# A recurrence kept in flight for two chunks at once: grouping its small matrix products on TensorE

## The chip, the cores and the metric

The kernel runs on one core of one Trainium2 chip. The metric is the time of one execution on the device in microseconds (us). Five engines work side by side, each through its own queue in order: PE (TensorE, matrix products), DVE (VectorE), ACT (ScalarE), POOL (GpSimd) and SP (SyncE, which issues most transfers). PEld in a row is TensorE's loading of weights.

## The reference, cut to what matters

One layer of a diffusion backbone runs over 1024 latent and 128 context tokens of width 1024: a feed-forward half step, a token mixer, a second feed-forward half step, a last norm. The mixer has attention and, beside it, a gated linear recurrence (HGRN2) that runs forwards and backwards over the tokens in 8 heads of 64 keys and 64 values. Everything is float32.

```python
# S_t = diag(f_t) S_{t-1} + k_t outer v_t,  o_t = S_t^T q_t,  k_t = 1 - f_t, chunkwise
q_h = silu(hq);  f_fw = lb0 + (1 - lb0) * sigmoid(hf_f);  f_bw likewise
o_fw, s_fw = hgrn2_chunked(q_h, 1 - f_fw, log(f_fw), v_h, s0[:, 0])
o_bw, s_bw = hgrn2_chunked(flip(q_h), flip(1 - f_bw), flip(log(f_bw)), flip(v_h), s0[:, 1])
o_rec = rmsnorm(o_fw + flip(o_bw), hg_norm_g) * silu(hgate)
merged = sigmoid(ga) * (o_attn @ w_up_attn) + sigmoid(gr) * (o_rec @ w_up_rec)
```

## The kernel before

**The dense products.** A float32 product is made of three products of split operands (high and low parts: `xh`, `xl`, `wh`, `wl`; lines 454 to 456). In the mixer, `dense_g` makes one output tile of 128 rows by 384 tokens from eight blocks of the inner dimension, in two halves of 12 matrix products each, with a `yield` between. Such a half is the unit in which the rest is dealt out. All 1152 tokens are three chunks of 384 (`ORDER` is 2, 0, 1). The generators `proj_f`, `proj_q`, `proj_v`, `proj_gate` and `proj_sg` make the projections of the mixer: forget gates per head, queries, values and output gates per pair of heads, and sigmoid gates that go to memory.

**The recurrence.** Each head and chunk (24 in all) goes through two generators. `scan_pre` makes decays and scaled keys and queries (`Kb`, `Qb`, `KE`, `QP`) on DVE, ACT and POOL. `scan_lev` makes the part inside 128-token tiles by levels: first the products inside blocks of 8 (level 0, `Kb` with `Qb`), then a level for each m of 8, 16, 32, 64, in which keys of one half of a block of 2m meet queries of the other half. The forward direction lies on partitions 0 to 63, the backward one on 64 to 127. For m of 8 and 16, one product over all 128 partitions covers both directions, because `kr[m]` holds zeros where a direction has no keys. For level 0 and for m of 32 and 64 there are two products over 64 partitions, one for each direction, into two banks. After each level, `KE` (DVE) and `QP` (DVE for the backward direction, POOL for the forward one) are multiplied by the decays of that level, ACT copies the next keys into `kr`, and ACT or DVE moves the products out. Then come `kt` (the transposes of `KE`) and `dS` (the change of state). `scan_out` runs the state `S` over the nine tiles of a head on DVE and makes the outputs `po`. The products of the levels lie in three banks (tag `lv`), those of `kt`, `dS`, `po`, `vt` (transposed values) and `ops` (the norm of a pair's output) in three more (`sm`), and the dense ones in two (`mm`).

**The order.** A scheduler keeps close to the order in which the program is written. The main loop takes one chunk after the other and puts one half of a projection behind each step of `scan_lev`:

```python
for _ in self.scan_lev(d, b):
    next(work, None)      # a half of a projection: 12 dense products
    next(pre, None)       # a step of scan_pre for the next chunk
```

**The entry.** The first feed-forward step ends in `down_last`, chunk after chunk; the norm of the third chunk (`norm`, the generator `self.tail`) is still to be done when the mixer starts, and is dealt out between the first projections (`weave(feed(0))`). `mixer_consts` makes the constants of the mixer there, with a transfer of `mask` from ACT's queue.

Of the kernel before, what the change touches and what calls it, by code (L numbers as in the profile page):

```python
# [19 lines left out]
P = 128  # L20
# [6 lines left out]
CW = 384  # L27
# [61 lines left out]
class Trunk:  # L89
# [3 lines left out]
    def run(self):  # L93
        self.part, self.mode, self.chunks, self.bg = {}, "ffn1", ORDER, iter(())
        nc, tc, a = self.nc, self.tc, self.a
        with ExitStack() as st:
            self.cp = st.enter_context(tc.tile_pool(name="cp", bufs=1))
            self.wp = st.enter_context(tc.tile_pool(name="wp", bufs=1))
            self.tp = st.enter_context(tc.tile_pool(name="tp", bufs=25))
# [10 lines left out]
            with tc.tile_pool(name="mp", bufs=1) as mp:  # L110
                self.mixer_consts(mp)
                self.mixer()
# [268 lines left out]
    def norm(self, c, i):  # L381

        nc = self.nc
        lo, hi = span(c)
        cs = slice(lo, hi)
        rs = self.rs[:, cs]
        if self.mode != "mix":
            rs = self.bank("ps1", "rsp", hi - lo)
        self.stat_end(c, rs)
        yield  # L390
        for k in range(KT):
            t = self.fp.tile([P, hi - lo], F32, tag=self.nt[0], bufs=self.nt[1], name="xn")
            nc.vector.tensor_mul(t, self.x[k][:, cs], rs)
# [11 lines left out]
            nc.gpsimd.tensor_sub(tl, t, th)  # L405
            yield
# [205 lines left out]
    def mixer_consts(self, cp):  # L612
        nc, a = self.nc, self.a
        self.mask = cp.tile([P, 4, G], U8, name="mask")
        mf = self.tt(F32, "maskf")[:, : 4 * G]
        nc.scalar.dma_start(mf, a["mask"])
        nc.vector.tensor_copy(self.mask.rearrange("p a b -> p (a b)"), mf)
# [36 lines left out]
    def proj_f(self, i, h, out):  # L654
# [3 lines left out]
        w = self.load_w(self.a["w_in"][i], KT, P, home="pieces" if i == 0 else "low")  # L658
        for c in ORDER:
            s = self.sigm((yield from self.proj_g(w, c)))  # L660
            lo, hi = c * CW, (c + 1) * CW
            for r, o in ((slice(0, 64), 0), (slice(64, P), 1)):
                nc.scalar.activation(
                    fs[r, lo + o : hi + o], s[r], AF.Identity, scale=self.lb1[r, h : h + 1], bias=self.lb[r, h : h + 1]
                )
            yield

    def proj_q(self, i, out):
        q = out["q"] = self.tt(F32, "q")
        w = self.load_w(self.a["w_in"][i], KT, P, home="low")  # L670
        for c in ORDER:
            ps = yield from self.proj_g(w, c)
            self.nc.vector.tensor_mul(q[:, c * CW : (c + 1) * CW], ps, self.sigm(ps))  # L673
            yield

    def proj_v(self, i, out):
        nc = self.nc
        V = out["V"] = self.tt(F32, "V")
        w = self.load_w(self.a["w_in"][i], KT, P, home="low")
        for c in ORDER:  # L680
# [3 lines left out]
            pt = self.pp.tile([P, CW], F32, tag="sm", bufs=3, name="vt")  # L684
            for j in range(3):
                nc.tensor.transpose(pt[:, ts(j, P)], t[:, ts(j, P)], self.ident)
            nc.scalar.copy(V[:, c * CW : (c + 1) * CW], pt)
            yield

    def proj_gate(self, i, p, oT):  # L690
        nc = self.nc
        w = self.load_w(self.a["w_in"][i], KT, P, home="low")
        sq = self.tt(F32, "osq")[:, :T]
        nc.scalar.activation(sq, oT[:, :T], AF.Square)
        for c in ORDER:
            ps = yield from self.proj_g(w, c)
            if c == ORDER[0]:
                self.lnexp()
                for b in ORDER:
                    self.rec_norm(b, oT, sq)  # L700
            s = self.sigm(ps)
            nc.vector.tensor_mul(s, ps, s)
            cs = slice(c * CW, (c + 1) * CW)
            nc.gpsimd.tensor_mul(s, oT[:, cs], s)
            nc.sync.dma_start(self.orec[p][:, cs], s)
# [9 lines left out]
    def hgrn(self):  # L715
        nc = self.nc
# [9 lines left out]
        for t in self.XY:  # L726
            nc.vector.memset(t[:, :, 3:4], 1.0)
        for t in self.A1 + [self.A2, self.kr[8], self.kr[16]]:
            nc.vector.memset(t, 0.0)
        self.cnt = 0  # L730
# [11 lines left out]
        for i, _ in enumerate(weave(feed(0))):  # L742
            if i < 12:
                next(self.tail, None)
            if i == 11:
                assert next(self.tail, 1)
        def scan_of(h):
# [4 lines left out]
            d.update(pairs[p])  # L752
# [4 lines left out]
        def work_of(h):  # L757
            p = h // 2
            work = feed(h + 1) if h + 1 < H else []
            if h and h % 2 == 0:  # L760
                work = [self.proj_gate(5 * p - 1, p - 1, pairs[p - 1]["o"])] + work
            while len(work) < 4:
# [3 lines left out]
        d = scan_of(0)  # L766
        for _ in self.scan_pre(d, ORDER[0]):
            pass
        for h in range(H):
            work = work_of(h)  # L770
            for n, b in enumerate(ORDER):
                nd, pre = None, iter(())
                if n < NCH - 1:
                    pre = self.scan_pre(d, ORDER[n + 1])
                elif h + 1 < H:
                    nd = scan_of(h + 1)
                    pre = self.scan_pre(nd, ORDER[0])
# [7 lines left out]
            for _ in work:  # L785
                pass
            oT, d = d["o"], nd
        for _ in self.proj_gate(19, 3, oT):
            pass

# [3 lines left out]
    def scan_pre(self, d, b):  # L794
        nc = self.nc
        fs, q, QP, hh = d["f"], d["q"], d["QP"], d["h"] % 2
# [23 lines left out]
        Kb, Qb, KE = tmp("Kb", 2), tmp("Qb", 2), tmp("KE", 2)  # L820
# [20 lines left out]
    def scan_lev(self, d, b):  # L841
        nc = self.nc
        V, QP, hh, Gall = d["V"], d["QP"], d["h"] % 2, d["Gall"]
# [3 lines left out]
        if b == ORDER[0]:  # L847
            d["dS"] = self.fp.tile([P, 9, 64], F32, tag="dS", bufs=1, name="dS")
            S = d["S"] = self.fp.tile([P, 8, 64], F32, tag="S", bufs=1, name="S")
# [6 lines left out]
        Af = d["As"][b] = tmp("Af", 4, (P, 3, P))  # L856
# [5 lines left out]
        def products(parts, k, q, blocks):  # L862
            for j in range(3):
                kj, qj = k[:, ts(j, P)], q[:, ts(j, P)]
                for ki, qi in blocks:
                    for r, ps in parts:
                        ks, qs = (ki, qi) if r != B else (qi, ki)
                        n = qs.stop - qs.start
                        nc.tensor.matmul(ps[ks, j, :n], kj[r, ks], qj[r, qs], start=True, stop=True)
# [16 lines left out]
        for li, m in enumerate((8, 16, 32, 64)):  # L886
            kr = self.kr[m]
            if m < G:
                ps = lv()
                products([(slice(0, P), ps)], kr, qp, diag)  # L890
            else:
                pair = (A, lv()), (B, lv())
                blocks = [(slice(u, u + m), slice(u + m, u + 2 * m)) for u in range(0, P, 2 * m)]
                products(pair, kr, qp, blocks)
# [16 lines left out]
            else:  # L911
                for u, v in blocks:
                    nc.scalar.copy(Af[u, :, v], pair[0][1][u, :, :m])
                    nc.scalar.copy(Af[v, :, u], pair[1][1][v, :, :m])
# [12 lines left out]
        yield  # L927
        pd = self.pp.tile([P, 3, 64], F32, tag="sm", bufs=3, name="dS")
# [5 lines left out]
        yield  # L934

    def scan_out(self, d):
        nc = self.nc
        h, V, QP, Gall, S, dS = d["h"], d["V"], d["QP"], d["Gall"], d["S"], d["dS"]
# [8 lines left out]
        for pairs, lows, highs in (((3, 4), (2, 5)), (2, 4), (4, 6)), (((1, 6), (0, 7), (8,)), (0, 2), (6, 9)):  # L947
# [9 lines left out]
            for half, (t0, t1) in ((A, lows), (B, highs)):  # L957
                pv = po[half, : t1 - t0].rearrange("p a b -> p (a b)")
                nc.scalar.copy(d["o"][r, t0 * P : t1 * P], pv)
# [652 lines left out]
    def ffn_fast(self, l, gm, nxt):  # L1612
# [93 lines left out]
        if l == 0:  # L1706
            self.bg = self.ada_sum((6, 7), lambda: self.bank("up", "cb", D // 2), partial(self.tt, F32), self.slim)
# [133 lines left out]
```

## Time and profile before

| what | value |
|---|---|
| time, median of 3 runs | 2933.15 us (2932.75 to 2934.38) |
| time of the profiled execution | 2932.25 us, of which the span in the trace is 2930.1 us |
| PE busy in the span | 2833.2 us (97%) |
| DVE, ACT, POOL busy | 1976.7, 1285.9, 957.3 us |
| first projections of the mixer to the last of its recurrence | from about 832 to 1456 us of the span |

A busy time is the sum of what an engine's instructions took; the ends of matrix products are modelled and overlap, so what PE really needs for a piece of work is read from the starts of its products in the timeline. A granted clock (PEclk) below 1 means that TensorE was slowed for a part of the stretch.

### The profile page before, as it was taken

The numbers are of one execution on the slowest core, as the hardware profiler recorded it, in microseconds if no ns is written. First come the engines' busy times: TensorE is split into PE (matmuls) and PEld (weight loads), VectorE is DVE, ScalarE is ACT, GpSimd is POOL, SyncE is SP. The second block draws the span as 40 slices with busy tenths as digits, with TensorE's granted clock in tenths as the row PEclk, the third lists the DMA queues.
The fourth block names the chain that finished last, engine by engine and source line by source line (L and its number), as shares of the span: only waits on it lengthen the run. The fifth ranks groups of instructions, "written<-read, shape, count | busy, mean of one in ns | idle before, by whom it ended". The sixth has DMA issues, their size and how long they took to land. (4 is left out here: it accounts for less than half of the span.)

```text
span 2930.1 us, 54396 instructions
## 1 busy us (share of the span) xinstructions
PE 2833.2 (97%) x20946; PEld 2668.0 (91%) x20946; DVE 1976.7 (67%) x4282; ACT 1285.9 (44%) x2574; POOL 957.3 (33%) x904
## 2 busy tenths in 40 slices
PE   6999999999999999999998999999999999999998
PEld 5999999999988888888996877699999999999997
DVE  7677777677678777777357777856665665556665
ACT  6432323321176666666536777721552332232112
POOL 0133322444132122222145444532342222235431
PEclk9999999999999999999998999999999999999999
DMA  6643333643111111111200001242542322235211
GB/s 245 206 146 122 122 127 111 255 162 119 61 61 66 40 55 42 55 42 53 73 31 14 16 18 34 74 163 72 165 147 93 108 83 75 75 120 199 92 46 65
DMA packets 151492, 282.44 MB, mean 96 GB/s; under 512 B 19201, under 2 KB 83777, under 8 KB 151233
## 3 DMA queue, kind: packets, MB, share of 16 engines
q1 hardware_dynamic: 151088, 278.90, 27.8%
q8 instruction: 165, 2.70, 0.4%
q14 instruction: 95, 0.77, 0.1%
q10 hardware_dynamic: 144, 0.07, 0.0%
HBM read 215.37 MB, written 63.52 MB: 95 GB/s over the span
## 5 line engine op out<-in xcount | busy, mean ns | idle before, releaser
L1590 PE MATMUL b<-xo,wo 128*128 128x288 f32 x3552 | 484.6, 296 | 0.0
L1590 PEld LDWEIGHTS b<-xo,wo 128*128 128x128 f32 x3552 | 476.4, 188 | 0.0
L483 DVE SCALAR_TENSOR_TENSOR x<-dn,modt,x 128x256 f32<-128x256 f32 (+4 forms) x728 | 353.3, 505 | 169.0 <-PE dn L456 168.1
L454 PE MATMUL mm<-xh,wh 128*128 128x384 f32 (+1 forms) x1008 | 363.5, 361 | 5.7 <-DVE q L673 3.7
L1590 PE MATMUL b<-bh,wo 128*128 128x288 f32 x1776 | 366.4, 295 | 0.6 <-ACT et L1600 0.6
L456 PE MATMUL mm<-xh,wl 128*128 128x384 f32 (+1 forms) x1008 | 342.8, 340 | 0.3 <-DVE wl L228 0.2
L455 PE MATMUL mm<-xl,wh 128*128 128x384 f32 (+1 forms) x1008 | 342.3, 340 | 0.0
L1590 PEld LDWEIGHTS b<-bh,wo 128*128 128x128 f32 x1776 | 289.2, 188 | 0.9 <-ACT et L1600 0.9
L1590 PE MATMUL b<-bl,wo 128*128 128x288 f32 x888 | 261.9, 295 | 0.0
L243 POOL TENSOR_TENSOR wl<-raw,wh 128x1024 fp32r<-128x1024 f32 (+3 forms) x71 | 152.0, 2142 | 267.8 <-ACT wh L242 265.0
L1565 ACT CAST wo<-raw 128x512 fp32r<-128x512 f32 x185 | 114.7, 621 | 229.5 <-PE b L1590 119.3
L454 PEld LDWEIGHTS mm<-xh,wh 128*128 128x128 f32 (+1 forms) x1008 | 189.8, 188 | 19.6 <-DVE q L673 4.3
L1566 DVE TENSOR_TENSOR wo<-raw,wo 128x512 fp32r<-128x512 f32 x185 | 127.1, 688 | 104.8 <-ACT wo L1565 101.9
L454 PE MATMUL dn<-hh,wh 128*128 128x384 f32 (+2 forms) x576 | 196.2, 341 | 1.3 <-DVE et L1606 0.8
L456 PE MATMUL dn<-hh,wl 128*128 128x384 f32 (+2 forms) x576 | 194.6, 338 | 1.0 <-POOL wl L243 1.0
L455 PE MATMUL dn<-hl,wh 128*128 128x384 f32 (+2 forms) x576 | 194.2, 337 | 0.0
L455 PEld LDWEIGHTS mm<-xl,wh 128*128 128x128 f32 (+1 forms) x1008 | 190.4, 189 | 1.9 <-issue 0.4
L456 PEld LDWEIGHTS mm<-xh,wl 128*128 128x128 f32 (+1 forms) x1008 | 189.9, 188 | 1.8 <-DVE wl L228 0.5
L1668 POOL TENSOR_TENSOR hl<-hr,hh 128x1152 fp32r<-128x1152 f32 x44 | 118.0, 2693 | 194.5 <-ACT hh L1667 100.7
L314 DVE SCALAR_TENSOR_TENSOR junk<-wada,cb 128x512 bf16<-128x512 f32 x224 | 165.0, 737 | 7.1 <-DMA wada<-in_w_aT 6.3
L1322 POOL TENSOR_TENSOR ehl<-e,ehl 128x512 fp32r<-128x512 f32 x93 | 122.6, 1323 | 141.7 <-ACT ehl L1320 78.8
L1590 PEld LDWEIGHTS b<-bl,wo 128*128 128x128 f32 x888 | 167.4, 189 | 0.0
(391 smaller groups left out, 6904.2 us busy)
## 6 DMA issues: line engine op xcount, KB each, us to landing
raw<-in_w SPq DMA_DIRECT2D x148, 256.0 KB, 3.2
raw<-in_w SPq DMA_DIRECT2D x58, 512.0 KB, 3.5
wada<-in_w_aT SPq DMA_DIRECT2D x112, 256.0 KB, 2.9
hr<-hs SPq DMA_DIRECT2D x44, 576.0 KB, 5.2
hs<-et SPq DMA_DIRECT2D x148, 144.0 KB, 1.7
raw<-in_w_in SPq DMA_DIRECT2D x41, 512.0 KB, 3.2
hb<-hd SPq DMA_DIRECT2D x44, 288.0 KB, 3.5
x<-in_xT SPq DMA_DIRECT2D x16, 576.0 KB, 6.4
```

What stands on the lines that cost most here:

```text
L243: pin((eng or self.nc.gpsimd).tensor_sub(wl, raw, wh))
L314: nc.vector.scalar_tensor_tensor(junk, ws[n % 2], 1.0, cs[s], ALU.mult, ALU.mult, accum_out=o)
L454: pin(nc.tensor.matmul(ps, wh, xh, start=start and i == 0, stop=False))
L455: pin(nc.tensor.matmul(ps, wh, xl, start=False, stop=False))
L456: pin(nc.tensor.matmul(ps, wl, xh, start=False, stop=stop and i == n - 1))
L483: nc.vector.scalar_tensor_tensor(self.x[m][:, a:b], ps[:, a - lo : b - lo], self.modt[:, gm, m, s : s + 1], self.x[m][:, a:b], ALU.mult, A ...
L1322: eng.tensor_sub(el, e, eh)
L1565: nc.scalar.copy(wh, src[i])
L1566: nc.vector.tensor_sub(wl, src[i], wh)
L1590: nc.tensor.matmul(ps, w[:, k], x[:, k, :QW], start=first, stop=last, skip_group_check=home != i)
L1668: nc.gpsimd.tensor_sub(hl, raw, hh)
```

## The change

It changes the mixer's recurrence and its entry; the arithmetic of the outputs is the same.

- **Two chunks in flight.** The main loop has a turn for each chunk. In a turn the new chunk (`cur`) does level 0 and levels 8 and 16, and the chunk before it (`old`) does levels 32 and 64, `kt` and `dS`. Small products are issued in three groups per turn (`group`), with 3, then 2 or 3, then 2 halves of projections between (`slots`). The outputs `po` of a head, the transposes of `V` (`turn_v`) and the norm of a pair's output are put into those groups too (`later`).
- **Full-row tiles at levels 32 and 64.** One product over all 128 partitions and one bank instead of two products over 64 and two banks. For this `kr[32]` and `kr[64]` are cleared at the start too. ACT's copies of these products stand right behind them.
- **More buffers** for that: `KE` 3, `dS` and `S` 2, `Af` 6, and 27 large tiles (`tp`) instead of 25.
- **The mixer's entry.** `mixer_consts` is called in the first feed-forward step, with its transfer on SP's queue. For the third chunk's norm DVE makes x·g·rs and later the low part in two `scalar_tensor_tensor`, and ACT adds the shift and rounds in one instruction; before, it was one on DVE, two on ACT and one on POOL. Its statistics have a higher priority. The first weights of `q` and `v` are split in two pieces. The first chunk's `scan_pre` starts among the first projections.

```diff
+            if last:                       # norm, mode "mix"
+                for a, b, s in segs(c):
+                    v, th, tl = t[:, a - lo : b - lo], self.xh[k][:, a:b], self.xl[k][:, a:b]
...
+                    nc.vector.scalar_tensor_tensor(v, self.x[k][:, a:b], g, rv, ALU.mult, ALU.mult)
+                    nc.scalar.activation(th, v, AF.Identity, bias=sh)
+                    nc.vector.scalar_tensor_tensor(tl, v, sh, th, ALU.add, ALU.subtract)
...
+    def group(self, *steps):
+        for s in steps:
+            if s is not None:
+                next(s, None)
+        later, self.later = self.later, []
+        for f in later:
+            f()
...
-                for _ in self.scan_lev(d, b):
-                    next(work, None)
-                    next(pre, None)
-                for _ in pre:
-                    next(work, None)
-            for _ in self.scan_out(d):
-                next(work, None)
...
+        for p in range(H * NCH + 1):
+            h, n = divmod(p, NCH)
+            old, cur, pre = cur, None, iter(())
+            if h < H:
+                cur = self.scan_lev(d, ORDER[n])
...
+            self.group(old, cur)
+            slots(3)
+            self.group(old, cur, old, out)
+            slots(2 + p % 2)
+            self.group(cur, out, old)
+            out = None
+            if p and n == 0:
+                out = self.scan_out(last if h < H else d)
+                next(out)
+            slots(2)
...
         for li, m in enumerate((8, 16, 32, 64)):
-            if m < G:
-                ps = lv()
-                products([(slice(0, P), ps)], kr, qp, diag)
-            else:
-                pair = (A, lv()), (B, lv())
+            ps = lv()
+            blocks = diag
+            if m >= G:
                 blocks = [(slice(u, u + m), slice(u + m, u + 2 * m)) for u in range(0, P, 2 * m)]
-                products(pair, kr, qp, blocks)
+                blocks = [c for k, q in blocks for c in ((k, q), (q, k))]
+            products([(slice(0, P), ps)], self.kr[m], qp, blocks)
+            if m >= G:
+                for k, q in blocks:
+                    nc.scalar.copy(Af[k, :, q], ps[k, :, :m])
...
-                for u, v in blocks:
-                    nc.scalar.copy(Af[u, :, v], pair[0][1][u, :, :m])
-                    nc.scalar.copy(Af[v, :, u], pair[1][1][v, :, :m])
```

**What moves on PE, in the recurrence.** `kr_9029` to `kr_9032` of the kernel before are the keys of levels 8, 16, 32, 64; each line of three dots stands for dense products (`mm`), twelve unless said otherwise. Before, one chunk is:

```order
L869 MATMUL lv<-Qb,Kb 32x32 x24
...
L869 MATMUL lv<-QP,kr_9029 32x32 x12
...
L869 MATMUL lv<-QP,kr_9030 32x32 x12
...
L869 MATMUL lv<-QP,kr_9031 32x32 x12
...
L869 MATMUL lv<-QP,kr_9032 64x64 x6
...
L924 MATMUL kt<-ident,KE 128x128 x3
...
L932 MATMUL dS<-V,kT 64x64 x6
```

After the change, with `kr_9026` to `kr_9029` for the four levels, one turn is (the first dots are 36 dense products, the second 24 or 36):

```order
L932 MATMUL lv<-QP,kr_9028 32x32 x12
L932 MATMUL lv<-Qb,Kb 32x32 x24
...
L932 MATMUL lv<-QP,kr_9029 64x64 x6
L932 MATMUL lv<-QP,kr_9026 32x32 x12
L984 MATMUL kt<-ident,KE 128x128 x3
...
L932 MATMUL lv<-QP,kr_9027 32x32 x12
L994 MATMUL dS<-V,kT 64x64 x6
```

Seven visits to small products per chunk have become three, with the same products in them. (The trace counts each of these float32 products as two instructions.)

**What moves on DVE, at the mixer's entry.** `rt` and `rs` are the third chunk's statistics, `xn` its normed tiles, `q` the first query tile, which must be read out before PE may use that bank again. Before:

```order
L623 MEMSET onesq 128x128
...
L363 SCALAR_TENSOR_TENSOR rt<-nps,rs 128x384
...
L365 SCALAR_TENSOR_TENSOR rs<-rt,rs 128x384
L393 TENSOR_TENSOR xn<-x_6219,rs 128x384
L393 TENSOR_TENSOR xn<-x_6221,rs 128x384
L393 TENSOR_TENSOR xn<-x_6257,rs 128x384
L657 MEMSET fs 64x1
L617 CAST mask<-maskf 128x128
L393 TENSOR_TENSOR xn<-x_6259,rs 128x384
L673 TENSOR_TENSOR q<-mm,sg 128x384
```

After:

```order
L361 SCALAR_TENSOR_TENSOR rt<-nps,rs 128x384
...
L363 SCALAR_TENSOR_TENSOR rs<-rt,rs 128x384
L401 SCALAR_TENSOR_TENSOR xn<-x_6219,gs,rs 128x384
L401 SCALAR_TENSOR_TENSOR xn<-x_6221,gs,rs 128x384
L401 SCALAR_TENSOR_TENSOR xn<-x_6257,gs,rs 128x384
L403 SCALAR_TENSOR_TENSOR xl_8447<-xn,modt,xh_8446 128x384
L403 SCALAR_TENSOR_TENSOR xl_8449<-xn,modt,xh_8448 128x384
L403 SCALAR_TENSOR_TENSOR xl_8451<-xn,modt,xh_8450 128x384
L401 SCALAR_TENSOR_TENSOR xn<-x_6259,gs,rs 128x384
L403 SCALAR_TENSOR_TENSOR xl_8453<-xn,modt,xh_8452 128x384
L687 TENSOR_TENSOR q<-mm,sg 128x384
```

The clears and the cast of `mask` no longer stand ahead of `q`; four low parts stand there instead.

More of the change, by code (lines that the diff above doesn't have):

```diff
@@ L388, in norm @@
             rs = self.bank("ps1", "rsp", hi - lo)
-        self.stat_end(c, rs)
+        last = self.mode == "mix"
+        if last:
+            with self.tc.high_priority(offset=600):
+                self.stat_end(c, rs)
+        else:
+            self.stat_end(c, rs)
         yield
@@ L683, in proj_v, with turn_v, proj_gate @@
             nc.scalar.copy(t, ps)
[L684 to L687, printed above, removed]
+            self.later.append(partial(self.turn_v, out, c, t))
             yield
-    def proj_gate(self, i, p, oT):
+    def turn_v(self, out, c, t):
+        pt = self.pp.tile([P, CW], F32, tag="sm", bufs=3, name="vt")
+        for j in range(3):
+            self.nc.tensor.transpose(pt[:, ts(j, P)], t[:, ts(j, P)], self.ident)
+        self.nc.scalar.copy(out["V"][:, c * CW : (c + 1) * CW], pt)
+        out["nv"] = out.get("nv", 0) + 1
+    def group(self, *steps):
[5 more added lines that the diff above has]
+            f()
+    def proj_gate(self, i, p, pair):
         nc = self.nc
+        oT = pair["o"]
+        assert pair["no"] == 4
         w = self.load_w(self.a["w_in"][i], KT, P, home="low")
@@ L725, in hgrn @@
         self.A2 = f32("A2", [P, 3, G])
[L726 to L730, printed above, removed]
+        self.cnt, self.later = 0, []
         heads = [{} for _ in range(H)]
@@ L751, in scan_of @@
             d = heads[h]
-            d.update(pairs[p])
+            d["pair"] = pairs[p]
             d["h"], d["QP"], d["As"] = h, self.tt(F32, "QP"), {}
@@ L760, in work_of @@
             if h and h % 2 == 0:
[L761 to L762 removed]
+                work = work + [sgs.pop(), sgs.pop()] + [self.proj_gate(5 * p - 1, p - 1, pairs[p - 1])]
+            while len(work) < 4 - (h == 3) + (h == H - 1):
                 work.append(sgs.pop())
             return chain(*work)
[L766 to L778 removed]
+        pre = iter(())
@@ new lines, in hgrn @@
+        for i, _ in enumerate(weave(feed(0))):
+            if i < 12:
+                next(self.tail, None)
+            if i == 11:
+                assert next(self.tail, 1)
+                for t in self.XY:
+                    pin(nc.vector.memset(t[:, :, 3:4], 1.0))
+                d = scan_of(0)
+                pre = self.scan_pre(d, ORDER[0])
+            if i == 13:
+                for t in self.A1 + [self.A2] + list(self.kr.values()):
+                    pin(nc.vector.memset(t, 0.0))
+            next(pre, None)
@@ new lines, in hgrn, with slots @@
+        for _ in pre:
+            pass
+        self.group()
+        work = chain.from_iterable(map(work_of, range(H)))
+        old = cur = out = last = None
+        for p in range(H * NCH + 1):
[3 more added lines that the diff above has]
+                cur = self.scan_lev(d, ORDER[n])
+            if p + 1 < H * NCH:
+                h1, n1 = divmod(p + 1, NCH)
+                while min(heads[h1].get("nf", 0), pairs[h1 // 2].get("nq", 0)) <= n1:
+                    next(work)
+                if n1 == 0:
+                    last, d = d, scan_of(h1)
+                pre = self.scan_pre(d, ORDER[n1])
+            def slots(k):
+                for _ in range(k):
@@ L791, in tmp @@
+            out = None
[3 more added lines that the diff above has]
+            slots(2)
+            for _ in pre:
+                pass
+        self.group(out, out)
+        for _ in work:
+            pass
+        for n, _ in enumerate(self.proj_gate(19, 3, pairs[3])):
+            if n == 0:
+                self.group()
     def tmp(self, n, bufs=1, sh=(P, CW)):
@@ L927, in scan_lev @@
         yield
+        V = d["pair"]["V"]
+        assert d["pair"]["nv"] > ORDER.index(b)
         pd = self.pp.tile([P, 3, 64], F32, tag="sm", bufs=3, name="dS")
```

87 lines of the change are left out of this document (46 added, 41 removed).

## The prediction, made before the changed kernel was run

> **What bounds the kernel now.** I read the page's first part, then busy time by stage, then PE's timeline inside the recurrence, and last its list of waits.
>
> ```profile
> span 2930.1 us, 54396 instructions
> PE 2833.2 (97%) x20946; PEld 2668.0 (91%) x20946; DVE 1976.7 (67%) x4282; ACT 1285.9 (44%) x2574; POOL 957.3 (33%) x904
> ...
> 820.00:876.00 56.00, 51.27 (x267) 48.26 (x265) 38.94 (x86) 43.27 (x88) 22.98 (x26) 0.94 0.16 55
> 876.00:1456.50 580.50, 556.29 (x6212) 494.75 (x6211) 412.93 (x1055) 369.19 (x872) 124.32 (x197) 0.99 0.16 53
> ...
> 876.00:1456.50 580.50, 468.14 (x2358) 405.54 (x2357) 10.88 (x20) 48.91 (x100) 0.99 0.16 53
> ```
>
> The columns of a stage are its length, then busy time and count of PE, PEld, DVE, ACT and (but in the last row, which holds the dense products `mm` alone) POOL, then the granted clock. The recurrence takes 580.5 us, and PE is idle in 24.2 of them (580.5 - 556.29). DVE is busy 71%. So PE sets the pace, and what the change can win lies in three places: waits of PE, the price of going from dense to small products and back, and the entry (820 to 876), where PE is idle 4.7 us and the clock is at 0.94.
>
> The timeline (start, length, engine, line, product, count) prices the visits:
>
> ```profile
> 1097.42 0.34 PE L454 MATMUL mm<-xh,wh 128*128 128x384 f32 x1
> 1097.60 0.34 PE L455 MATMUL mm<-xl,wh 128*128 128x384 f32 x1
> 1097.77 0.34 PE L456 MATMUL mm<-xh,wl 128*128 128x384 f32 x1
> 1098.04 0.62 PE L869 MATMUL lv<-Qb,Kb 64*32 64x32 f32 x48
> 1098.59 0.44 PE L454 MATMUL mm<-xh,wh 128*128 128x384 f32 x1
> 1098.87 0.34 PE L455 MATMUL mm<-xl,wh 128*128 128x384 f32 x1
> ...
> 1100.62 0.34 PE L456 MATMUL mm<-xh,wl 128*128 128x384 f32 x1
> 1100.89 0.40 PE L869 MATMUL lv<-QP,kr 128*32 128x32 f32 x24
> 1101.22 0.44 PE L454 MATMUL mm<-xh,wh 128*128 128x384 f32 x1
> 1101.50 0.34 PE L455 MATMUL mm<-xl,wh 128*128 128x384 f32 x1
> ...
> 1111.28 0.34 PE L456 MATMUL mm<-xh,wl 128*128 128x384 f32 x1
> 1111.45 0.49 PE L924 MATMUL kt<-ident,KE 128*128 128x128 f32 x3
> 1111.69 0.42 PE L454 MATMUL mm<-xh,wh 128*128 128x384 f32 x1
> 1111.95 0.34 PE L455 MATMUL mm<-xl,wh 128*128 128x384 f32 x1
> ...
> 993.02 0.34 PE L456 MATMUL mm<-xh,wl 128*128 128x384 f32 x1
> 993.28 0.52 PE L869 MATMUL lv<-Qb,Kb 64*32 64x32 f32 x36
> 993.92 0.55 PE L686 MATMUL vt<-ident,t 128*128 128x128 f32 x3
> 994.40 0.28 PE L869 MATMUL lv<-Qb,Kb 64*32 64x32 f32 x12
> 994.61 0.44 PE L454 MATMUL mm<-xh,wh 128*128 128x384 f32 x1
> 994.89 0.34 PE L455 MATMUL mm<-xl,wh 128*128 128x384 f32 x1
> ```
>
> Dense products start every 0.175 us (1097.42, 1097.60, 1097.77); the printed length is a modelled one. From the last dense product ahead of a visit to the second one behind it, two pitches (0.35) would pass without the visit. So a visit costs:
> - level 0, 48 instructions: 1098.87 - 1097.77 - 0.35 = 0.75 us;
> - level 8, 24 instructions: 1101.50 - 1100.62 - 0.35 = 0.53 us;
> - `kt` alone: 1111.95 - 1111.28 - 0.35 = 0.32 us;
> - level 0 with three transposes in its midst: 994.89 - 993.02 - 0.35 = 1.52 us.
>
> From 0.75 and 0.53, 24 small instructions cost 0.22, and the visit itself 0.53 - 0.22 = 0.31 us. Part of that is seen at each end: 1100.89 - 1100.62 - 0.175 = 0.095 at the way in, 1101.50 - 1101.22 - 0.175 = 0.105 for the second dense product behind. `kt`, whose tiles have the dense shape, pays no such part (three of 0.11). And 1.52 is 0.45 more than 0.75 + 0.32: two changes of shape inside a visit, 0.22 each.
>
> **Part 1, fewer visits.** The order shows seven visits per chunk becoming three: level 32 with level 0, level 64 with level 8 and `kt`, level 16 with `dS`. That is three merges of small with small per chunk, 72 in all, and 24 `kt` that now stand behind small products. Each merge saves 0.31 less the change between two small shapes, which no row shows. Its ends are 0 (saving 0.31) and the 0.22 between small and full shape (saving 0.09). I take 0.10, nearest to the 0.095 of the way in, because what the 0.22 holds beyond that is a full-size load of weights that small tiles don't need. Saved: 72 x 0.21 = 15.1 us (6.5 to 22.3). `kt` behind small products costs 0.22 at its start, less the 0.105 that the dense product behind the group no longer pays: 24 x 0.12 = 2.9 us lost (0 to 5.3). Half of the 16 visits of `po` join `dS`, which has their shape: 8 x 0.31 = 2.5 us saved. The other half follow `kt` and change nothing. The number of products, and of tiles at levels 32 and 64, stays. Sum: 15.1 - 2.9 + 2.5, so 15 us saved (4 to 25).
>
> [...]
>
> **Part 2, the waits in the recurrence.**
>
> ```profile
> PE lv L869 <- ACT Af L913: 10.3, 9, 1.6
> PE dS L932 <- ACT kT L926: 3.4, 4, 1.0
> ...
> 1079.26 0.33 PE L869 MATMUL lv<-QP,kr 64*64 64x64 f32 x2
> 1081.05 0.56 PE L869 MATMUL lv<-QP,kr 64*64 64x64 f32 x10 [1.47 <-ACT Af L913]
> ...
> 1037.30:1046.50 9.20, 7.62 (x48) 6.83 (x47) 6.80 (x14) 7.74 (x20) 2.66 (x3) 0.81 0.12 44
> 1324.60:1333.80 9.20, 7.62 (x47) 6.82 (x46) 6.78 (x14) 7.74 (x20) 2.69 (x3) 0.81 0.13 45
> ...
> L905 DVE TENSOR_TENSOR QP<-QP,T 64x192 f32<-64x192 f32 x96 | 43.5, 453 | 25.6 <-PE lv L869 23.7
> L905 POOL TENSOR_TENSOR QP<-QP,T 64x192 f32<-64x192 f32 x96 | 59.4, 619 | 152.3 <-PE lv L869 152.3
> ```
>
> Of the 24.2 us idle, 10.3 come from level 64: its first bank is free, its second is one that level 32 filled and ACT has not yet copied (1079.26, then 1.47 us of waiting). With one bank per level, a chunk takes six turns of the three banks instead of eight, and two or three halves lie between: 2 x 12 x 0.175 = 4.2 us, where it was 2.1. The same 4.2 us stand between products and the next group that needs `QP`, whose update takes 0.45 us on DVE and 0.62 on POOL, and between `kt` and `dS` (3.4 us of waits now). `KE` for the transposes no longer has a half between, but its update needs no product of its own group and stands nearly a turn earlier in DVE's queue. Three times (two rows shown) the clock falls to 0.81 over 9.2 us around a wait, 1.75 us lost each, 5.2 in all. What goes at most is 24.2 + 5.2 = 29 us. What stays I take as 8 us: the norm of a pair's output still stands on ACT and DVE ahead of the copies at three places (2 us each, against 3.4 now), and 2 for the rest. Saved: 21 us (5 to 29).
>
> [...]
>
> **Part 3, the entry.**
>
> ```profile
> 836.81 0.91 PE L438 MATMUL nps<-rs,ones 128*128 128x384 f32 x2 [1.59 <-DVE rs L379]
> 853.16 0.69 PE L454 MATMUL mm<-xh,wh 128*128 128x384 f32 x1 [2.48 <-DVE q L673]
> ...
> 849.80 1.04 DVE L617 CAST mask<-maskf 128x128 uint8<-128x128 f32 x1 [1.25 <-DMA maskf<-in_mask]
> ...
> L393 DVE TENSOR_TENSOR xn<-x,rs 128x384 f32<-128x384 f32 x8 | 5.0, 653 | 3.2 <-POOL xl L405 1.9 <-PE vt L686 1.3
> ```
>
> 4.7 us idle and 0.06 x 56 = 3.4 us of clock make 8.1. The wait of 2.48 is for `q`, and ahead of `q` DVE waits 1.25 for the transfer of `mask` and casts it for 1.04; both go. The wait of 1.59 for the last sum of squares stays. DVE makes eight tiles more (8 x 0.65 = 5.2 us); its idle 17 us of that stage (56 - 38.94) hide them, and if they didn't, `q` would be late by four of them, 2.6 us, which is the old wait again. The cleared keys of levels 32 and 64 and the moved clears lie in the same idle time. The transfer of `mask` on SP's queue and its cast stand among the feed-forward's work, long before its use; if DVE waits for it there as here, 1.25 us, PE has full banks to go on with, and without them it costs that. I take 4 us saved (0 to 7).
>
> Buffers that are deeper cost nothing by themselves; the rest of the program keeps its order.
>
> **The sum.** 2932.25 (the profiled execution: 2930.1 of span and 2.15 around it) - 15 - 21 - 4 = 2892. The median of the runs is 0.9 above that execution, so 2893.
>
> **The rivals.**
> - [...] Chance 0.12.
> - *Waits change their place.* Groups wait for the latest of their members, and the 29 us stay under new names: 2933 - 15 - 4 = 2914. For: three points at which all must be ready instead of seven. Against: twice the distance. Chance 0.12.
> - *DVE becomes late, and the kernel slower.* DVE's work per chunk is 412.93 / 24 = 17.2 us and the turn shrinks from 24.2 to about 22.5. `QP` of two chunks now stands in one queue with `KE` of a third, and every group needs a `QP`. If old waits went and the 72 groups each waited 1 us for `QP`: 2933 - 15 - 4 - 29 + 72 = 2957. It turns slower from 48 / 72 = 0.67 us per group on. For: DVE's `KE` updates stall on ACT's copies ahead of `QP`. Against: `QP` follows its products in the queue at once, 4.2 us stand between, and DVE idles 168 us of 580.5. Chance 0.11.
>
> That the change doesn't do what it says is excluded by the order, which shows the groups.
>
> **How the numbers follow.** The forecast, 2893, has 0.63; its own ends are 2932 - 25 - 29 - 7 = 2872 (with the 0.9, rounded) and 2932 - 4 - 5 = 2924. The first two rivals lie inside, only the third outside above. Trimming the upper end, where all three terms would have to fail at once, the range is 2870 to 2921. The remaining 0.02 is something not thought of. A measurement of this kernel tells about 0.2%, 6 us, from no change: 2927 or less is faster. All but the third rival give that, less a little for waits that nearly eat the gain: faster 0.86, same 0.03, slower 0.11.
>
> **What would show it.** Right: PE's idle time in the recurrence falls from 24 us to under 10, waits of `lv` for `Af` vanish, the stage from the first projection to the last `po` shrinks by 35 to 40 us, groups of small products cost 1.0 to 1.2 us (level 32 with 0). Wrong: many waits of `lv` for `QP` or `kr` of half a microsecond and more, DVE busy over 90% of the stage, changes of shape inside a group above 0.2 us, or a clock below 0.99 in the stage.

## The result, and the profile after

The change takes 2896.7 us (median of 4 runs, 2893.57 to 2898.68) where the kernel before takes 2933.4 on the same chip: a ratio of 0.9877, 95% interval 0.9865 to 0.9889, 36.7 us less. The profiled execution took 2896.2 us. Below, first the page of the kernel after (span, busy time), then its stages: length, busy time and count of PE, PEld, DVE, ACT, POOL, then the granted clock. The last two rows are the two places in the recurrence where the clock still falls, each 3.41 us long.

```profile
span 2894.2 us, 54329 instructions
...
PE 2803.6 (97%) x20946; PEld 2665.0 (92%) x20946; DVE 1967.4 (68%) x4292; ACT 1278.4 (44%) x2566; POOL 943.4 (33%) x896
```

```profile
820.00:876.00 56.00, 51.14 (x272) 49.15 (x271) 44.04 (x94) 41.31 (x83) 16.18 (x19) 0.94 0.16 58
876.00:1416.70 540.70, 526.55 (x6194) 490.46 (x6193) 397.90 (x1052) 360.85 (x868) 118.29 (x196) 0.99 0.16 56
884.08:887.49 3.41, 3.41 (x13) 3.41 (x12) 3.30 (x12) 1.37 (x3) 0.00 (x0) 0.50 0.44 154
1116.18:1119.59 3.41, 3.41 (x46) 2.79 (x44) 3.29 (x8) 1.79 (x3) 0.88 (x1) 0.50 0.02 5
```

PE is idle in 14.2 us of the recurrence (540.7 - 526.55), where it was 24.2. To see where the time came from I use three marks of PE's timeline: the last product of the feed-forward step (`dn`), the first product of a level (`lv`), and the last projection ahead of attention (`mm`, then `kps`). Of before, then of after:

```profile
832.01 0.34 PE L456 MATMUL dn<-hh,wl 128*128 128x384 f32 x1
882.23 0.62 PE L869 MATMUL lv<-Qb,Kb 64*32 64x32 f32 x48
1543.60 0.34 PE L456 MATMUL mm<-xh,wl 128*128 128x384 f32 x1
```

```profile
833.00 0.34 PE L469 MATMUL dn<-hh,wl 128*128 128x384 f32 x1
880.59 0.54 PE L932 MATMUL lv<-Qb,Kb 64*32 64x32 f32 x38
1508.70 0.34 PE L469 MATMUL mm<-xh,wl 128*128 128x384 f32 x1
```

The **entry** (`dn` to `lv`) went from 50.2 to 47.6 us, the **stage** (`lv` to the last `mm`) from 661.4 to 628.1. Together 35.9 us; what lies before became 1.0 longer and what lies behind 1.0 shorter. Both stages hold the same 2808 dense products (491.4 us at 0.175). The rest I split with the prediction's own measure (starts around a visit, less two pitches): the cost of the visits themselves (the shortest visit of each kind, that is of the same products in the same order, times its count) fell from 136.0 to 119.6 us; waits and slow clock beyond that fell from 34.0 to 17.1. A kind that occurs once counts with its wait, so the split is good to a few microseconds.

The three kinds of group in PE's timeline of the kernel after:

```profile
1001.68 0.34 PE L469 MATMUL mm<-xh,wl 128*128 128x384 f32 x1
1001.95 0.40 PE L932 MATMUL lv<-QP,kr 128*32 128x32 f32 x24
1002.27 0.62 PE L932 MATMUL lv<-Qb,Kb 64*32 64x32 f32 x48
1002.83 0.44 PE L467 MATMUL mm<-xh,wh 128*128 128x384 f32 x1
1003.11 0.34 PE L468 MATMUL mm<-xl,wh 128*128 128x384 f32 x1
...
1139.61 0.34 PE L469 MATMUL mm<-xh,wl 128*128 128x384 f32 x1
1139.88 0.89 PE L932 MATMUL lv<-QP,kr 128*64 128x64 f32 x36
1140.70 0.55 PE L984 MATMUL kt<-ident,KE 128*128 128x128 f32 x3
1141.01 0.42 PE L467 MATMUL mm<-xh,wh 128*128 128x384 f32 x1
1141.27 0.34 PE L468 MATMUL mm<-xl,wh 128*128 128x384 f32 x1
```

Level 32 with level 0 costs 1003.11 - 1001.68 - 0.35 = 1.08 us, where 0.53 and 0.75 were paid before; level 64 with level 8 and `kt` costs 1.31, the sum of three visits was 0.69 + 0.52 + 0.32 = 1.53. What PE still waits for from 820 to 1420 us (total, times, longest):

```profile
PE mm L467 <- DVE sg L742: 4.6, 4, 1.8
PE nps L451 <- DVE rs L377: 4.5, 1, 4.5
PE mm L467 <- DVE q L687: 4.3, 3, 2.3
PE vt L705 <- ACT t L698: 2.9, 3, 1.6
PE lv L932 <- DVE QP L969: 1.4, 1, 1.4
```

No level waits for `Af` any more. What is left stands mostly in front of dense products, whose two banks DVE gives back late. These waits are largely new: over the whole stage they were 1.8 us before (1.2 for `q`, 0.6 for `sg`) and are 10.3 now, while the waits of levels and of `dS` fell from 19.3 to 2.1.

### The profile page after: what moved, and what is told of

Its sections match the earlier page's. It is cut to its first block, busy times and chain, and to the rows that moved or that the text cites. A ratio compares the mean times of both kernels' runs of the same rounds, so it can differ in the third digit from the quotient of the medians.

```text
span 2894.2 us, 54329 instructions
## 1 busy us (share of the span) xinstructions
PE 2803.6 (97%) x20946; PEld 2665.0 (92%) x20946; DVE 1967.4 (68%) x4292; ACT 1278.4 (44%) x2566; POOL 943.4 (33%) x896
## 5 line engine op out<-in xcount | busy, mean ns | idle before, releaser
L467 PE MATMUL mm<-xh,wh 128*128 128x384 f32 (+1 forms) x1008 | 352.1, 349 | 10.8 <-DVE sg L742 6.0
```

The costliest lines, as they stand in the source:

```text
L467: pin(nc.tensor.matmul(ps, wh, xh, start=start and i == 0, stop=False))
```

## The experiments

Eleven further runs, each beside runs of the kernel before. Entry and stage are read from the profile by the marks above. The clock's falls in the stage differ between two executions of one program (two in the change, three in the change again, 1.7 us of clock each; the mean granted clock of the two profiled executions is 0.989 and 0.987), so 2 us of stage between two profiles tell little.

| kernel | time, us | ratio to before, 95% interval | entry | stage |
|---|---|---|---|---|
| before | 2933.4 | | 50.2 | 661.4 |
| the change | 2896.7 | 0.9877 (0.9865 to 0.9889) | 47.6 | 628.1 |
| before, full-row tiles alone | 2930.2 | 0.9990 (0.9981 to 0.9999) | 51.0 | 656.2 |
| change, two banks | 2925.9 | 0.9979 (0.9970 to 0.9988) | 47.6 | 659.0 |
| change, groups split | 2915.2 | 0.9939 (0.9926 to 0.9951) | 47.6 | 643.1 |
| change, split and two banks | 2926.7 | 0.9976 (0.9966 to 0.9986) | 47.6 | 655.7 |
| change, near groups | 2905.2 | 0.9905 (0.9890 to 0.9920) | 47.6 | 634.3 |
| change, no priority | 2899.4 | 0.9883 (0.9866 to 0.9899) | 48.8 | 628.0 |
| change, old norm | 2902.8 | 0.9894 (0.9879 to 0.9909) | 52.0 | 628.6 |
| change, QP on DVE | 2897.3 | 0.9879 (0.9864 to 0.9894) | 47.6 | 627.9 |
| change, tables kept together | 2898.1 | 0.9878 (0.9863 to 0.9893) | 47.6 | 629.9 |
| change, gate ahead of the norm | 2891.0 | 0.9856 (0.9843 to 0.9870) | 47.7 | 622.1 |
| the change, again | 2897.6 | 0.9878 (0.9863 to 0.9894) | 47.6 | 627.9 |

**The bank alone.**

```diff
-                pair = (A, lv()), (B, lv())
...
-                products(pair, kr, qp, blocks)
+                blocks = [c for k, q in blocks for c in ((k, q), (q, k))]
+            products([(slice(0, P), ps)], self.kr[m], qp, blocks)
```

The order is that of the kernel before.

> The kernel before, with full-row tiles at levels 32 and 64 alone (one product over 128 partitions and one bank for each; the keys of the other direction cleared once); order, entry and everything else as before. Theory: the 10.3 us in which products of a level waited for ACT's copies (Af) vanish, because six turns of the three banks are left where there were eight, and of the 5.2 us of half clock about a third goes with them: 10 to 13 us less than before, 2920 to 2923 us; group costs and visits stay (level 32 at 0.53, level 64 at 0.50). Rival (waits change their place): the same time stands under other names, 2930 to 2934. Rival (bank and grouping help only together): 2933, with the Af waits still there.

It gave 5.2 us in the stage and 0.1% in all, a quarter of what I expected. PE's waits:

```profile
PE lv L868 <- DVE QP L902: 12.4, 19, 1.2
PE dS L928 <- ACT kT L922: 7.9, 7, 1.3
```

The `Af` waits are gone, and `QP` and `kT` have taken their place: at 2.1 us between levels the next thing was late at once. So here the rival (waits change their place) is right. PE's waits in the stage did not fall at all (22.7 us before, 24.8 here); of the 5.2 us gained, 3.4 are two falls of the clock that are missing in this profile (mean granted clock 0.991, 0.989 before).

**The groups with two banks.** The same edit backwards, in the changed kernel.

> The changed kernel with levels 32 and 64 put back to two products over 64 partitions and two banks each; groups and distances as changed. The first group then needs four banks of three, and the order shows the second half of level 0 two to ten dense products further back. Theory: the full-row tiles are what lets two levels stand in one group; without them each turn pays one more visit (0.31 us) and a wait for ACT's copies of about 0.7 us (up to 1.6, the longest Af wait of before): 24 x 1.0 = 24 us more than the change, 2921 us (2904 to 2943). Rival (the gain is in the visits and their distance, the bank is a side matter): the 10.3 us of bank waits return and no more, 2907 or less, and the merges keep their 0.20 us each.

The stage is 30.9 us longer than with full rows, nearly the whole gain. Waits are 16.5 us more, and slow clock 13.7 (mean granted clock 0.985, 0.989 in the change; its cost overlaps with that of the waits). The first group needs four banks of three, and PE's timeline shows it waiting in the middle of level 0:

```profile
900.43 0.39 PE L933 MATMUL lv<-Qb,Kb 64*32 64x32 f32 x24
905.55 0.55 PE L933 MATMUL lv<-Qb,Kb 64*32 64x32 f32 x24 [4.18 <-ACT Af L959]
```

**The merges alone.**

```diff
-            self.group(old, cur)
-            slots(3)
+            solo(cur)
+            slots(1)
+            self.group(old)
+            slots(2)
```

The lines are those of the first group; the other two are split in the same way.

> The changed kernel with each of the three groups of a turn split in two, half a projection (12 dense products) between the two members; the distances from a level to the next one of the same chunk stay two or three halves, banks stay as changed. Only the merges are undone. Theory: each of the 72 merges saved 0.20 us (0.10 for an inner change of shape against 0.31 for a visit of its own): 14.5 us more than the change, 2911 us, with new visits of level 0 at 0.75 and level 8 at 0.53 and PE's idle time in the recurrence within 3 us of 14. Rival (full price of inner changes, all gain is in waits): a merge saves 0.09, 2903. Rival (merging saves nothing, waits are all): 2897.

The stage is 15.0 us longer (expected 14.5), the whole 18. In its timeline the two visits stand apart:

```profile
984.87 0.34 PE L469 MATMUL mm<-xh,wl 128*128 128x384 f32 x1
985.14 0.40 PE L943 MATMUL lv<-QP,kr 128*32 128x32 f32 x24
...
985.75 0.34 PE L468 MATMUL mm<-xl,wh 128*128 128x384 f32 x1
...
1008.07 0.34 PE L469 MATMUL mm<-xh,wl 128*128 128x384 f32 x1
1008.34 0.62 PE L943 MATMUL lv<-Qb,Kb 64*32 64x32 f32 x48
...
1009.17 0.34 PE L468 MATMUL mm<-xl,wh 128*128 128x384 f32 x1
```

0.53 and 0.75 apart, 1.08 together: a merge saves 0.20. By the shortest cost of every kind the three merges save 0.198, 0.194 and 0.192, 14.0 us for 72. Some 7 us of new waits of `vt` for ACT stand against smaller waits of dense products, so the split isn't clean to the microsecond; the group costs are.

**Split groups with two banks.** Both edits together.

> The split groups (half a projection between the two members of each group) with levels 32 and 64 on two products over 64 partitions and two banks each; the distances of the change, no merges, no full-row tiles. It shows whether the bank is needed for the distance or only for two levels in one group. Theory (only for the group): at 2.1 us between level 0 and level 32 most copies are done in time, 0 to 10 us more than the split groups, 2915 to 2925. Rival (needed for two chunks in flight at all): the 31 us that two banks cost in the grouped order come here too, 2945.

The bank costs 12.6 us of stage here (643.1 to 655.7), a little over the theory, and 30.9 where two levels stand in one group. It matters for two chunks in flight, and over twice as much for the merge.

**The distance alone.**

```diff
-            slots(3)
+            slots(1)
...
-            slots(2 + p % 2)
+            slots(1)
...
-            slots(2)
+            slots(5 + p % 2)
```

> The changed kernel with the same groups, but one half of a projection between the first and second and the second and third group of a turn (2.1 us, the distance of before) and five or six behind the third; merges, banks and tiles as changed. Theory (the distance is needed once two levels stand in a group, since DVE has about 1.5 us of updates for each level and each group now waits for two levels): waits of lv for QP, kr and Af of 0.5 to 1 us return in most of 48 near groups, 24 to 40 us more, 2921 to 2937. Rival (only the bank and the merges matter; at 2.1 us the kernel before waited for QP hardly ever): 2897 to 2901, PE's idle time as in the change, 14 us.

6.2 us of stage: between the theory and the rival, and far under my 24. Two rows of its waits show what the distance covers: the norm of a pair and eight late `QP`. At the norm, `kt` waits for a bank: the norm's sums `ops` hold all three banks that they share with `kt`, and `rt` is DVE's reading of the first. It isn't `KE` that is late, since the last update of any `KE` had ended at 1068.65 us, a microsecond before the first of these waits began:

```profile
PE kt L984 <- DVE rt L361: 5.7, 3, 2.2
PE lv L932 <- DVE QP L969: 5.1, 8, 1.7
```

**The entry.** First without the priority of the last statistics (`with self.tc.high_priority(offset=600)` removed), then with the whole norm of the third chunk as before (`last = False`), which takes the priority away too.

> The changed kernel without the higher priority of the last statistics at the mixer's entry: PE then makes 12 dense products of the mixer before the sum of squares of the third chunk (nps), as the kernel before did, instead of waiting for it first. Theory: the wait in front of nps falls from 4.5 us to the 1.6 us of the kernel before, 2.9 us less than the change, 2894 us; if the 6.8 us of half clock behind that wait go too, 2891. Rival (the norm of the third chunk is what the entry waits for): what PE gains ahead of nps it waits for later, at q or at the first level, 2896 to 2899.

> The changed kernel with the third chunk's norm as before (no higher priority, and one instruction on DVE, two on ACT, one on POOL per tile instead of two on DVE, one on ACT); the constants' earlier place, the split weights and the earlier first scan_pre stay. Theory (the entry's gain is that q no longer stands behind the mask on DVE): as without the priority alone, 2894 us. Rival (the gain is in the shorter norm of three instructions): its last tiles come 2 to 4 us later and PE waits for them, 2898 to 2901.

Without the priority, PE makes 12 dense products ahead of `nps` and waits 1.6 us there instead of 4.5, and the first level still comes 1.2 us later: the rival is right, the third chunk's norm is what the entry waits for. With the old norm as well it comes another 3.2 us later, at 52.0, longer than before the change, though the mask, the split weights and the early `scan_pre` were left as changed; why it is longer than before is not shown. The first wait for a dense bank, in the change and with the old norm:

```profile
849.98 0.45 PE L467 MATMUL mm<-xh,wh 128*128 128x384 f32 x1 [0.40 <-ACT sg L664]
```

```profile
851.05 0.69 PE L467 MATMUL mm<-xh,wh 128*128 128x384 f32 x1 [4.73 <-ACT sg L664]
```

The sigmoid that gives the bank back stands on ACT behind the norm's tiles. Without the priority alone, this wait was 2.25. So the shorter norm (one ACT instruction per tile instead of two) is worth 3.2 us of the entry, and its earlier start 1.2.

**DVE's reserve.**

```diff
-                (A, nc.gpsimd, qp, 1, tL),
+                (A, nc.vector, qp, 1, tL),
```

> The changed kernel with the forward half of each QP update on DVE instead of POOL: 96 instructions of about 0.4 us, 40 us more for DVE in the recurrence (398 to about 440 of 541 us, 81%), nothing else. It prices the reserve that DVE has. Theory (two or three halves, 4.2 to 6.3 us, between a group and the next that needs its QP are enough): 0 to 6 us more than the change, 2897 to 2903. Rival (DVE is near its limit, the prediction's slower case): half a microsecond of waiting at each of 72 groups, 36 us more, 2933.

```profile
876.00:1416.70 540.70, 525.55 (x6194) 489.38 (x6193) 418.07 (x1152) 361.63 (x869) 61.69 (x99) 1.00 0.17 56
```

DVE is 20 us busier (half of what I expected of 96 instructions) and the stage doesn't move: 627.9, with 1.0 us more of waits and one fall of the clock less than in the change. 20 us more on DVE are free here.

**What is left: ACT's tables or DVE's queue.** At the norm of a pair ACT changes its function table up to six times, 1.28 us each (ACT's timeline of the change, the first of six from 1064.34 to 1074.49):

```profile
1064.34 1.28 ACT L359 ACT_TABLE_LOAD   x1
```

First I kept the logarithms and exponentials together:

```diff
+            load = nc.scalar.preload_act_table_set("natural_log_exp_and_others")
+            self.behind(load, self.lastsig)
...
+            self.exps = [nc.scalar.activation(sq[:, cs], sq[:, cs], AF.Exp, scale=-0.5) for cs in sl]
...
+        for e in self.exps:
+            self.behind(i, e)        # i: the next sigmoids
```

> The changed kernel with the six logarithms and exponentials of the norm of a pair's output kept together on ACT, behind the sigmoids written before them and ahead of those written after; the order then has two loads of ACT's function tables (1.28 us each) at each of the four norms instead of five or six; nothing else moves. Theory (what is left of the waits hangs on ACT at these places): the stalls of about 2 us at the norms, 1070 and 1329 us of the span, go, 4 to 6 us less than the change, 2891 to 2893. Rival (DVE's run of twelve instructions of the norm, 6 us in its queue, is what makes the gate's sg late): 2896 to 2898, the same waits for DVE.

ACT is 19.5 us less busy (360.85 to 341.35 in the same stretch), and nothing is gained. The timelines of this kernel say why: ACT's last sigmoids, DVE's queue and PE's wait. On DVE, L745 to L748 are the norm, L761 the gate's product that gives a dense bank back:

```profile
1070.54 0.87 ACT L664 ACTIVATE sg<-mm 128x384 f32<-128x384 f32 x2
```

```profile
1072.60 0.55 DVE L745 SCALAR_TENSOR_TENSOR rt<-ops,osq 128x384 f32<-128x384 f32 x1
...
1074.06 0.55 DVE L761 TENSOR_TENSOR sg<-mm,sg 128x384 f32<-128x384 f32 x1
```

```profile
1074.66 0.69 PE L467 MATMUL mm<-xh,wh 128*128 128x384 f32 x1 [2.71 <-DVE sg L761]
```

The sigmoids had ended at 1071.4 (1070.54 + 0.87). So, with the tables still kept together, I moved the last three instructions of each chunk's norm behind that chunk's gate product (`gate`). This is an order on DVE's queue; `rt` also got three buffers of its own, because it lives longer. One of the three lines:

```diff
+            self.behind(nc.vector.scalar_tensor_tensor(t, t, -0.5, sq[:, cs], ALU.mult, ALU.mult), gate)
```

> The changed kernel with the logarithms and exponentials of a pair's norm kept together on ACT, and on DVE the last three instructions of each chunk's norm moved behind that chunk's gate product (sg), so that the gate's bank is given back ahead of them. Theory (DVE's queue, not ACT's tables, holds the bank: the sigmoid was ready at 1071.4 us of the span, and its product on DVE stood behind the norm's run until 1074.1): the waits of dense products for sg, 5 us, and the half clock behind them go, 4 to 7 us less than the change, 2890 to 2893 us, and from the first level to the last projection 621 to 624 us where the change takes 628.1. Rival (DVE's other work is as late, q or QP take the place of sg): 2896 to 2898, 628 us.

> The changed kernel once more, beside the other two on the same chip: 2895 to 2898 us, 628 us from the first level to the last projection.

2891.0 us (2889.9 to 2891.9) beside 2897.6 (2897.0 to 2898.8) for the change on the same chip: 6.6 us less, and the stage 5.9 us shorter. The gate's product comes at 1070.18. The rows below are that product, then the waits from the first level to the last projection in the change, run again, and in this version, then its recurrence with the clock at 1.00:

```profile
1070.18 0.56 DVE L762 TENSOR_TENSOR sg<-mm,sg 128x384 f32<-128x384 f32 x1 [0.53 <-ACT sg L664]
```

```profile
PE mm L467 <- DVE sg L742: 5.2, 3, 1.9
PE mm L467 <- DVE q L687: 3.9, 3, 1.9
```

```profile
PE mm L467 <- DVE q L694: 5.0, 4, 2.3
PE mm L467 <- DVE sg L762: 1.1, 1, 1.1
```

```profile
876.00:1416.70 540.70, 528.40 (x6214) 491.53 (x6213) 402.82 (x1056) 346.74 (x862) 118.48 (x196) 1.00 0.18 58
```

This version beats both kernels. The theory is right for `sg`, and the rival for a part: `q` waits 1.1 us more. All waits of PE in the stage fell only from 13.8 to 12.0 us. The larger part of the gain is the clock, three falls (5.1 us) in the change run again and none here (mean granted clock 0.987 and 0.992). Two of these stood behind waits for `sg` that are gone. The third stood behind the wait for `q`, which is no shorter here (2.32 us against 1.89): why it didn't slow the clock in this profile is not shown. The two profiles are also the slowest and the fastest of their four runs, so the 6.6 us of the medians are the better size.

## Why the prediction was right, and where its steps were off

It said 2893 and the runs gave 2896.7. Against the profiled execution it expected 40 us less (15, 21 and 4); the profile shows 35.9. The total is closer than its terms, since the visits gave more than forecast and the waits and the entry less.

- **Merges: right in size and mechanism.** 0.21 saved per merge was expected, 0.195 was measured, by the group costs and by the split groups (15.0 us). An inner change of shape thus costs 0.31 - 0.195 = 0.115 us, next to the 0.10 taken.
- **`kt` behind small products: wrong sign.** A loss of 2.9 us was expected. The shortest visit of level 64 with `kt` is 0.98 us (in the split groups), alone they were 0.69 and 0.33: 0.04 saved each time, 0.9 us in all. The 0.22 that the prediction read from transposes inside a visit of level 0 doesn't hold here, and that part of it is a full-size load of weights was my estimate, which no run shows (last section).
- **`po` with `dS`:** expected 2.5; 1.44 and 0.69 alone, 1.79 together, so 0.34 for each of 8, 2.7. Visits together: 14.0 + 0.9 + 2.7 = 17.6 where 15 was expected.
- **Waits: the step that was off.** 21 of 29 us were to go, 8 to stay. PE's idle time in the recurrence fell by 10.0, and the clock now costs 3.4 us (two falls of 3.41 us to 0.50) where it cost 5.2: 12 us, and 17.6 stay. What the visits leave of the stage's gain is 33.3 - 17.6 = 16; idle time goes by modelled ends, so the two need not agree. The mechanism was right for the levels: their waits and those of `dS` went from 19.3 to 2.1 us, and bank and distance belong together, since the bank alone turned into waits for `QP` and `kT`, and taking the distance away cost 6. What was mis-sized is the remainder. The prediction put 2 us at each of three norms on ACT and DVE "ahead of the copies"; what waits there, and at the queries, is the dense products' own banks, 10.3 us for `sg` and `q` where it was 1.8, a resource that it did not look at. The last experiment shows this for `sg`; for `q` (2.32 us at one place) it is read from DVE's queue alone.
- **The entry: near in size, wrong in mechanism.** 4 us expected, 2.6 measured. The mask's cast and transfer were to be the gain; with them gone and the old norm kept, the entry was 52.0, no shorter than before. The gain is the shorter norm (3.2 us) and its earlier start (1.2). "The wait of 1.59 stays" failed too: it became 4.46, and cost nothing, since without it the first level comes later.
- **The signs to look for.** Waits for `Af` vanished, the group of level 32 and 0 cost 1.08, and entry and stage shrank by 35.9, all as said; PE's idle time was to be under 10 us and is 14.2.
- **The rivals.** *Inner changes at 0.22* (the end of part 1's range at which a merge saves 0.09): shown wrong by the merges, which save 0.195. *Waits change their place*: right for the bank alone, and for the change in part: of the 17.2 us that levels and `dS` no longer wait, 8.5 came back in front of dense products. *DVE late*: 20 us more on DVE moved nothing, so the slower case was far off.

An inner change of shape was not free: at 0.115 us it is about a third of a visit's own 0.31. The clock fell behind single waits of 1.6 to 2.3 us: in the recurrence of the kernel before three times behind 1.58 us for `Af`, in that of the change behind 1.59 for `t` and 2.32 for `q`, each time to 0.50 for 3.41 us. So the prediction was right to hang the 5.2 us of slow clock on the waits, and too hopeful in letting them go: other waits brought back 3.4.

## What to carry to other kernels

Price a visit of small products from the starts of the dense ones around it; then merging visits can be forecast to a few hundredths of a microsecond, as here. When a wait is taken away, look what is due next at the same distance: the bank that gained 5 us alone was worth 31 beside the grouping, and the waits that went from the levels came back by half in front of dense products. Before an engine is blamed for a wait, read its queue: work that gives a bank back belongs ahead of work that nobody waits for. And before a few microseconds between two profiles are explained, count the falls of the clock in both.

## What the runs showed of the hardware

The same wait doesn't always slow the clock. In the change PE waits 2.32 us for `q`, and soon after the clock is at 0.50 for 3.41 us (from 1116.18 on, above). In the last version the same wait stands at the same place, to the hundredth, and the clock stays at 1.00. Below are the two waits, then the 3.41 us ahead of the fall in the change, and 5 us around and behind the wait's end in the last version:

```profile
1114.72 0.44 PE L467 MATMUL mm<-xh,wh 128*128 128x384 f32 x1 [2.32 <-DVE q L687]
```

```profile
1112.16 0.44 PE L467 MATMUL mm<-xh,wh 128*128 128x384 f32 x1 [2.32 <-DVE q L694]
```

```profile
1112.77:1116.18 3.41, 1.46 (x8) 1.46 (x9) 3.26 (x10) 1.03 (x2) 0.00 (x0) 1.00 0.00 0
```

```profile
1112.00:1117.00 5.00, 4.84 (x59) 4.49 (x60) 4.82 (x14) 2.78 (x5) 0.88 (x1) 1.00 0.01 3
```

The cleanest pair is one program, the change and the change again. Its wait for `sg` at the first norm is 1.81 us long in the first execution and 1.83 in the second, and the clock fell behind the second alone. Below are the wait of the first, whose recurrence has its two falls elsewhere (884.08 and 1116.18, above), then of the second the 3.41 us with the wait and the 3.41 us behind them:

```profile
1073.28 0.45 PE L467 MATMUL mm<-xh,wh 128*128 128x384 f32 x1 [1.81 <-DVE sg L742]
```

```profile
1073.26:1076.67 3.41, 1.58 (x41) 1.23 (x40) 2.83 (x6) 3.35 (x5) 0.34 (x1) 1.00 0.02 5
1076.67:1080.08 3.41, 3.41 (x13) 3.41 (x12) 2.42 (x5) 3.33 (x7) 1.62 (x3) 0.50 0.17 60
```

Ahead of the two falls in the recurrence of the change PE was idle for 1.59 and 1.95 of 3.41 us, and for 1.58 ahead of each of the three in the kernel before. So here the length of a wait did not tell by itself whether the clock fell; what else decided is not shown, as no run moved a wait by itself.

Transposes of full shape behind a group of small products cost no more than alone (0.98 us together, 0.69 and 0.33 apart). Inside a visit of level 0 the prediction read 0.22 us for each change of shape, half of the 0.45 by which 1.52 us exceeds 0.75 + 0.32. The weight loads of those transposes are idle for 0.23 us ahead of their first, though, and the trace puts that down to ACT's `t`:

```profile
993.92 0.31 PEld L686 LDWEIGHTS vt<-ident,t 128*128 128x128 f32 x3 [0.23 <-ACT t L683]
```

How much of the 0.45 belongs to the shape is open, as no run moved the transposes within a group.
